# Gates of a sparse expert layer kept column by column in groups of 16 tokens: matmuls write PSUM with a step of four, and the gates meet the activations in runs of 16

## The chip, the cores and the metric

The kernel runs on one core of a Trainium2 chip. The metric is the device time of one execution in microseconds, the median of several runs. A core has TensorE (PE, with its weight loads shown apart as PEld), VectorE (DVE), ScalarE (ACT), GpSimd (POOL) and SyncE (SP), which here only issues transfers. The four compute engines share the on-chip memory SBUF; matmuls write to a second one, PSUM, whose banks hold 512 float32 per partition.

## The reference: what is computed

One encoder layer for 256 tokens of width 2048 in float32: a retention group and a recurrent group, cross attention to 256 memory tokens, then a sparse expert layer (PEER), and a final norm. Only the expert layer matters here:

```python
sub_scores = jnp.einsum('thcd,hckd->thck', q, sub_keys)     # 8 heads, 2 x 128 keys
vals, ids = lax.top_k(sub_scores, 16)
top_sc, pos = lax.top_k(cand.reshape(t, 8, 256), 16)        # cand: all sums of two of them
eid = i1 * 128 + i2                                         # 128 experts for each token
gate = jax.nn.softmax(top_sc, axis=-1)
act = jax.nn.gelu(jnp.einsum('td,tkd->tk', xb, u_tab[eid]))
out = jnp.einsum('tk,tkd->td', gate * act, v_tab[eid])
```

There are 128 x 128 = 16384 experts, each with one row of `u_tab` and one of `v_tab`. A token uses 128 of them.

## The kernel before

The kernel computes the expert layer in two ways at once. The first 96 of 128 groups of experts (`RD` = 96, regrouped by key pair) are computed densely for all 256 tokens: for each expert the activation of every token, times a gate that is zero where the token did not choose the expert. The other 32 groups are computed by gathering only the chosen rows from DRAM. The dense part is cut into 12 chunks (`NCH`) of eight groups, which makes 8 x 128 experts a chunk, experts on the partitions.

*The bank of gates.* `gbuild` makes the gates for all experts of the dense part. It takes four tokens at a time. DVE writes two comparisons with a row of numbers, `o1` (128 entries by 128 first keys, line 876) and `o2` (128 entries by 96 groups, line 879), and ACT scales `o2` by the softmax weights (line 882). For each of the four tokens PE multiplies the two (line 892): the result, 128 partitions by 96 groups, is the token's gate for every dense expert. The four results fill 384 columns of one PSUM bank, token after token, so a column's place is (token, chunk, group in chunk). A copy takes them to the SBUF tile `gs`, which collects 16 tokens in the order (chunk, token, group); ACT and DVE take turns at the copies (line 894). After 16 tokens POOL issues one DMA of `gs` to the DRAM tensor `gd` (line 898), which holds for each chunk and partition 256 tokens by 8 groups. The matmuls are plain float32, which PE runs as two passes, so 256 of them leave 512 records. The last write of `gd` is issued at 1218 us.

*Where it runs.* `gbuild` and `compact` (which picks the rows to gather) are generators. They are pumped a little after each weight step while the first chunks' U products run (`u_chunk`, PE lines 129 and 131). A scheduler orders the instructions there.

*U and V steps.* From about 1200 us a hand-written list of steps rules (`run`). A U step multiplies half a block of `u_tab` with all tokens; two give the activations of one group, which go through `foldu` (ACT line 978, DVE line 982) and gelu (ACT line 987) into the tile `act` of the chunk. A V step multiplies activations with a piece of `v_tab` (lines 924, 925, 927). All weights are split in two for accuracy: ACT rounds the raw tile to `hi` (line 1048), DVE subtracts to get `lo` (line 1054), and line 131 or 927 uses `lo`. Chunks are computed six ahead (`LEAD`): for i = 0 to 5, sixteen V steps of chunk i are followed by sixteen U steps of chunk i + 6; then come the V steps of chunks 6 to 10 alone; `v_final` does chunk 11.

*The gates' steps.* `prep_steps` puts two steps per chunk into this list, one for each half of the tokens. Each loads 128 tokens' gates of the chunk from `gd` into a raw tile, as any weight is loaded (six tiles in turn, issued by SP, eight steps ahead, line 1043), and then DVE multiplies the activations by them in place (`gate`, line 1002). For this the tile, stored (token, group), is read as (group, token). Afterwards ACT and DVE split the gated activations into two (`ah`, `al`, or `xe`; lines 1016 and 1020) for PE.

*Gathered experts.* Between the steps `chosen` is pumped with a rate of 1.17 per step: POOL gathers rows (line 1094), and DVE takes dot products with them (line 1111) or adds multiples of them to the output `hh` (line 1119). Within one engine all of this is one fixed order, so a late instruction holds up all behind it.

Of the kernel before, what the change touches and what calls it, by code (L numbers as in the profile page):

```python
# [9 lines left out]
F32 = mybir.dt.float32  # L10
# [4 lines left out]
ALU = mybir.AluOpType  # L15
AX = mybir.AxisListType

P = 128
D = 2048
KB = D // P  # L20
T = 256
# [12 lines left out]
RD = 96  # L34
RS = P - RD
NS = RS * P
NCH = RD // 8
# [34 lines left out]
def hybrid_layer_kernel(ctx: ExitStack, tc: tile.TileContext, a: dict, out: bass.AP, dbg=None):  # L72
    nc = tc.nc
    V, A, G, PE = nc.vector, nc.scalar, nc.gpsimd, nc.tensor
# [6 lines left out]
    dp = ctx.enter_context(tc.tile_pool(name="dp", bufs=1, space=bass.MemoryType.DRAM))  # L81
# [11 lines left out]
    def bigx(name):  # L93
        return b8.tile([P, KB, 2 * T], F32R, tag="X", name=name, bufs=1)

    def slot(tag, shape, name, dt=F32):
        return b8.tile(shape, dt, tag=tag, name=name, bufs=3 if tag == "ms" else 2)
# [5 lines left out]
    def sm(name):  # L103
        return ps2_.tile([P, 512], F32, tag="sm", name=name)
# [307 lines left out]
    for i in range(3):  # L412
        t = slot("qs" if i == 0 else "ms", [P, TT, 1024], "qkv"[i])
# [448 lines left out]

    ring = []
    acts = {}
    gd = dp.tile([NCH, P, T, 8], F32, name="gd")

    def gbuild():
        prev = None
        gs = None
        for n in range(T // 4 + 1):  # L870
            nxt = None
            tt, t0 = divmod(4 * n, P)
            ss = slice(t0, t0 + 4)
            if n < T // 4:
                o1 = pgt.tile([P, 4, P], F32, tag="o1", name="o1", bufs=2)
                V.tensor_tensor(o1, iota[:, None, :].to_broadcast([P, 4, P]),
                                i1T[tt][:, ss, None].to_broadcast([P, 4, P]), op=ALU.is_equal)
                o2 = pgt.tile([P, 4, P], F32, tag="o2", name="o2", bufs=2)
                V.tensor_tensor(o2[:, :, :RD], iota[:, None, :RD].to_broadcast([P, 4, RD]),
                                rT[tt][:, ss, None].to_broadcast([P, 4, RD]), op=ALU.is_equal)  # L880
                for j in range(4):
                    A.activation(o2[:, j, :RD], o2[:, j, :RD], AF.Copy, scale=gtT[tt][:, t0 + j:t0 + j + 1])
                nxt = (o1, o2)
                yield 0.9
            if prev:
                o1, o2 = prev
                m = n - 1
                if m % 4 == 0:
                    gs = slot("qs", [P, NCH, 16, 8], "gs")
                pt = sm("G")  # L890
                for j in range(4):
                    PE.matmul(pt[:, j * RD:(j + 1) * RD], o1[:, j, :], o2[:, j, :RD], start=True, stop=True)  # L892
                g0 = 4 * (m % 4)
                (V.tensor_copy if m % 2 else A.copy)(
                    gs[:, :, g0:g0 + 4, :], pt[:, :4 * RD].rearrange("p (t c x) -> p c t x", t=4, x=8))
                if m % 4 == 3:
                    tl = slice(4 * m - 12, 4 * m + 4)
                    G.dma_start(gd[:, :, tl, :].rearrange("q p t c -> p q t c"), gs)
                yield 0.4
            prev = nxt  # L900
        done.add("gbuild")
# [95 lines left out]
    def prep_steps(i):  # L997
        box = []

        def gate(g, tt):  # L1000
            av = acts[i][:, :, tt * P:(tt + 1) * P]
            V.tensor_tensor(av, g.rearrange("p (t c) -> p c t", c=8), av, op=ALU.mult)

        def rounded(k):
            if k == 0:
                if NCH - LEAD < i < NCH - 1:
                    if "x" not in spare:
                        spare["x"] = bigx("xe").rearrange("p a b -> p (a b)").rearrange(
                            "p (n c e t) -> p n c e t", n=2, c=2, e=8)
                    box.extend((spare["x"][:, i % 2, 0], spare["x"][:, i % 2, 1]))  # L1010
                else:
                    box.append(tp.tile([P, 8, T], F32R, tag="ah", name="ah"))
                    box.append(tp.tile([P, 8, T], F32R, tag="al", name="al"))
                ahs[i] = box
            s = slice(4 * k, 4 * k + 4)
            A.copy(box[0][:, s], acts[i][:, s])

        def left(k):
            s = slice(4 * k, 4 * k + 4)
            V.tensor_tensor(box[1][:, s], acts[i][:, s], box[0][:, s].bitcast(F32), op=ALU.subtract)  # L1020

        for tt in range(TT):
            post = {}
            if tt == 1:
                post = {2: [(lambda: rounded(0), None)], 4: [(lambda: rounded(1), lambda: left(0))],
                        6: [(None, lambda: left(1))]}
            yield gd[i, :, tt * P:(tt + 1) * P, :].rearrange("p t c -> p (t c)"), lambda g, tt=tt: gate(g, tt), post

    def woven(main, extra, first, apart):
        main, extra = list(main), list(extra)  # L1030
# [267 lines left out]
    pgt = pg.__enter__()  # L1298
    done.add("pb")
    wv.add(turns(gbuild(), compact()))  # L1300
    wv.rate = RB
    for i in range(LEAD):
# [12 lines left out]
    wv.rate = RC  # L1315
    wv.add(chosen(blocks_of(0, 0, BASE) + blocks_of(1, 0, BASE), True))
    steps = woven(list(u_steps(LEAD - 1))[2 * CUT:], prep_steps(0), 6, 3)
    for i in range(NCH - 1):
        if i + LEAD < NCH:
            steps += woven(v_steps(i), [], 0, 0)  # L1320
            steps += woven(u_steps(i + LEAD), prep_steps(i + 1), 3, 4)
        else:
            steps += woven(v_steps(i), prep_steps(i + 1), 2, 4)
# [98 lines left out]
```

## Time and profile before

| | |
|---|---|
| median of 3 runs | 2084.04 us (2079.66 to 2085.44) |
| profiled execution | 2085.37 us, span 2083.4 us, granted clock 0.991 |
| busy over the span | PE 97%, PEld 82%, DVE 81%, ACT 49%, POOL 18% |
| gate matmuls, line 892 | 512 passes, 67.5 us busy, 272 ns mean |
| copies out of the bank, line 894 | DVE 32 of 551 ns, ACT 32 of 475 ns |
| gate multiplies, line 1002 | 24 of 2140 ns, 51.3 us of DVE |
| issue to landing | gates out 5.3 us, gates in 8.5 us, V tiles 7.4 us (medians) |

The page gives busy times for a whole span of unlike stretches, so the views by stretch and the waits inside a stretch say more. "Idle" of an engine is put down to what released it last. The matmuls are pipelined: a row's duration is longer than the distance from one start to the next, and the distance is the pace.

### The profile page before, as it was taken

To read this page: it belongs to the slowest core of one execution; us is meant where nothing else is said; L and a number is where in the kernel's file an instruction comes from. 1 tells how busy PE (TensorE), PEld (TensorE's weight loads), DVE (VectorE), ACT (ScalarE), POOL (GpSimd) and SP (SyncE) were. 2 spreads that over 40 slices of the span, in tenths; PEclk is the share of its full clock that TensorE was granted. 3 is DMA by queue.
4 is the path that set the end of the run, shared out by engine and by line. 5 is a ranking of instruction groups with operands and counts; after the bars stand their busy time and mean duration, and the time that the engine had idled before them with its cause. 6 is when DMAs were issued, how large, how long until landed. Compare 5 with 4: busy or idle time off the path is not lost.

```text
span 2083.4 us, 28880 instructions
## 1 busy us (share of the span) xinstructions
PE 2022.8 (97%) x10416; PEld 1717.1 (82%) x10416; DVE 1694.3 (81%) x2461; ACT 1031.2 (49%) x1570; POOL 375.4 (18%) x210
## 2 busy tenths in 40 slices
PE   8999999999999999999999988999999999999998
PEld 6888878888888888888789976888888888878776
DVE  6859766644554457999988888999999999999985
ACT  6565434544544455554558853435444453534443
POOL 0200020000000000000011022333433333534531
PEclk9999999999999999999999999999999999999999
DMA  8675645566654458555576579999999999999984
GB/s 288 235 242 173 215 132 185 172 191 188 190 172 142 142 182 284 171 176 180 162 255 207 181 266 349 403 392 397 375 351 340 388 390 387 387 393 351 336 303 132
DMA packets 132933, 541.94 MB, mean 260 GB/s; under 512 B 16677, under 2 KB 19365, under 8 KB 114597
## 3 DMA queue, kind: packets, MB, share of 16 engines
q1 hardware_dynamic: 108000, 387.90, 54.9%
q0 software_dynamic: 24784, 152.16, 18.8%
q8 instruction: 81, 1.33, 0.3%
q14 instruction: 68, 0.55, 0.1%
HBM read 537.80 MB, written 18.87 MB: 267 GB/s over the span
## 4 chain that ended last, share of the span: by engine, by line
PE 80%; DVE 12%; DMA 5%; issue 2%; ACT 1%; POOL 0%; SPq 0%; ACTq 0%; DVEq 0%; POOLq 0%
PE U L129 14%; PE U L131 7%; PE wb L129 7%; PE xc L171 6%; PE xc L172 6%; PE xc L174 6%; PE acc L927 6%; PE acc L925 5%; PE acc L924 5%; PE wb L131 4%; DVE lo L120 3%; PE G L892 2%; PE V L927 2%; DMA raw<-in_V_dram 2%; PE V L924 2%
## 5 line engine op out<-in xcount | busy, mean ns | idle before, releaser
L120 DVE TENSOR_TENSOR lo<-raw,hi 128x1024 fp32r<-128x1024 f32 x384 | 470.8, 1228 | 262.7 <-PE xc L174 118.4
L119 ACT CAST hi<-raw 128x1024 fp32r<-128x1024 f32 x384 | 403.1, 1051 | 305.0 <-PE xc L172 170.4
L1048 ACT CAST hi<-raw 128x1024 fp32r<-128x1024 f32 x284 | 296.2, 1049 | 261.8 <-DMA raw<-in_V_dram 100.9
L129 PE MATMUL U<-xn,hi 128*128 128x512 f32 x1536 | 404.6, 400 | 9.6 <-ACT hi L1048 4.2
L1054 DVE TENSOR_TENSOR lo<-raw,hi 128x1024 fp32r<-128x1024 f32 x284 | 341.4, 1221 | 29.1 <-ACT hi L1048 14.2
L129 PEld LDWEIGHTS U<-xn,hi 128*128 128x128 f32 x1536 | 279.1, 191 | 61.0 <-DVE foldu L982 6.5
L131 PEld LDWEIGHTS U<-xn,lo 128*128 128x128 f32 x1536 | 211.0, 192 | 20.9 <-DVE lo L120 5.5
L131 PE MATMUL U<-xn,lo 128*128 128x256 f32 x1536 | 220.1, 285 | 3.2 <-DVE lo L120 3.2
L1094 POOL DMA_INDIRECT gat<-in_Us_dram,idx x65 | 118.9, 1829 | 232.9 <-DVE gat L1111 218.2
L925 PE MATMUL acc<-hi,al 128*128 128x512 f32 x384 | 150.7, 393 | 7.3 <-DVE al L1020 7.3
L924 PE MATMUL acc<-hi,ah 128*128 128x512 f32 x384 | 151.3, 394 | 0.0
L1111 DVE SCALAR_TENSOR_TENSOR gat<-gat,h 128x2048 f32<-128x2048 f32 x65 | 148.5, 2285 | 0.0
L129 PE MATMUL wb<-hT,hi 128*128 128x512 f32 x448 | 119.8, 400 | 0.0
L1094 POOL DMA_INDIRECT gat<-in_Vs_dram,idx x40 | 81.5, 2038 | 125.8 <-DVE hh L1119 115.9
L927 PE MATMUL acc<-lo,ah 128*128 128x512 f32 x384 | 103.5, 392 | 0.0
L1094 POOL DMA_INDIRECT h<-in_Vs_dram,idx x30 | 81.3, 2709 | 102.4 <-DVE hh L1119 94.6
L129 PE MATMUL wb<-xT,hi 128*128 128x512 f32 x368 | 93.0, 394 | 1.2 <-ACT hi L119 1.2
L1119 DVE SCALAR_TENSOR_TENSOR hh<-gat,coef,hh 128x2048 f32<-128x2048 f32 x40 | 93.9, 2347 | 0.0
L129 PEld LDWEIGHTS wb<-hT,hi 128*128 128x128 f32 x448 | 81.3, 189 | 14.0
L925 PEld LDWEIGHTS acc<-hi,al 128*128 128x128 f32 x384 | 72.8, 189 | 23.8 <-DVE al L1020 8.2
L673 POOL DMA_DIRECT2D hn<-h x2 | 1.3, 658 | 487.3 <-DVE h L671 487.3
L927 PEld LDWEIGHTS acc<-lo,ah 128*128 128x128 f32 x384 | 72.7, 189 | 15.4 <-issue 0.2
(413 smaller groups left out, 3740.9 us busy)
## 6 DMA issues: line engine op xcount, KB each, us to landing
raw<-in_U_dram SPq DMA_DIRECT2D x192, 512.0 KB, 5.3
raw<-in_V_dram SPq DMA_DIRECT2D x192, 512.0 KB, 7.4
raw<-in_w_xyg_dram SPq DMA_DIRECT2D x48, 512.0 KB, 4.3
raw<-in_w_qkv_dram SPq DMA_DIRECT2D x48, 512.0 KB, 4.3
raw<-in_w_xk_dram SPq DMA_DIRECT2D x32, 512.0 KB, 3.6
raw<-in_w_xv_dram SPq DMA_DIRECT2D x32, 512.0 KB, 4.2
raw<-in_w_out_dram SPq DMA_DIRECT2D x32, 512.0 KB, 4.0
raw<-in_w_xq_dram SPq DMA_DIRECT2D x32, 512.0 KB, 3.5
```

Of the source, the lines that this page charges most:

```text
L119: A.copy(hi, raw)
L120: V.tensor_tensor(lo, raw, hi.bitcast(F32), op=ALU.subtract)
L129: PE.matmul(pt, hi[:, ks], xt[:, kb, :], start=(kb == 0), stop=(kb == KB - 1))
L131: PE.matmul(pt[:, :T], lo[:, ks], xt[:, kb, :T], start=False, stop=False)
L171: PE.matmul(pt, xh, hi[:, w], start=(n == 0 and k == 0), stop=False)
L924: PE.matmul(pt, ah[:, c, t_], hi[:, w], start=(first and c == 0), stop=False)
L925: PE.matmul(pt, al[:, c, t_], hi[:, w], start=False, stop=False)
L927: PE.matmul(pt, ah[:, c, t_], lo[:, w], start=False, stop=(last and c == 7))
L1048: A.copy(his[t], raws[t])
L1054: V.tensor_tensor(los[t], raws[t], his[t].bitcast(F32), op=ALU.subtract)
L1094: G.indirect_dma_start(gat, None, a[tab], bass.IndirectOffsetOnAxis(ap=idx[tt][:, k:k + 1], axis=0), bounds_check=NS - 1, oob_is_err=False)
L1111: V.scalar_tensor_tensor(gat, gat, 1.0, h[0], op0=ALU.mult, op1=ALU.mult, accum_out=dots[tt, k0][:, k:k + 1])
```

## The change

Three access patterns change, and with them the layout of the bank in PSUM, SBUF and DRAM. The four products of a bank are interleaved: token j of a matmul writes columns j, j + 4, j + 8 and so on, so a column's place in PSUM is now (chunk, group, token). The copy reads the 384 columns in a row, and writes four tokens at a time into `gs`, which is now (chunk, group, token of 16). `gd` holds for each chunk and partition 16 groups of tokens, each 8 groups of experts by 16 tokens. A gate multiply therefore reads its gates in runs of 16 neighbouring tokens; activations and output keep their places.

```diff
-    gd = dp.tile([NCH, P, T, 8], F32, name="gd")
+    gd = dp.tile([NCH, P, T // 16, 8, 16], F32, name="gd")
...
-                    gs = slot("qs", [P, NCH, 16, 8], "gs")
+                    gs = slot("qs", [P, NCH, 8, 16], "gs")
                 pt = sm("G")
                 for j in range(4):
-                    PE.matmul(pt[:, j * RD:(j + 1) * RD], o1[:, j, :], o2[:, j, :RD], start=True, stop=True)
+                    PE.matmul(pt[:, :4 * RD].rearrange("p (c t) -> p c t", t=4)[:, :, j], o1[:, j, :],
+                              o2[:, j, :RD], start=True, stop=True)
                 g0 = 4 * (m % 4)
                 (V.tensor_copy if m % 2 else A.copy)(
-                    gs[:, :, g0:g0 + 4, :], pt[:, :4 * RD].rearrange("p (t c x) -> p c t x", t=4, x=8))
+                    gs[:, :, :, g0:g0 + 4], pt[:, :4 * RD].rearrange("p (c x t) -> p c x t", t=4, x=8))
                 if m % 4 == 3:
-                    tl = slice(4 * m - 12, 4 * m + 4)
-                    G.dma_start(gd[:, :, tl, :].rearrange("q p t c -> p q t c"), gs)
+                    G.dma_start(gd[:, :, m // 4].rearrange("q p c t -> p q c t"), gs)
...
         def gate(g, tt):
-            av = acts[i][:, :, tt * P:(tt + 1) * P]
-            V.tensor_tensor(av, g.rearrange("p (t c) -> p c t", c=8), av, op=ALU.mult)
+            av = acts[i][:, :, tt * P:(tt + 1) * P].rearrange("p c (b t) -> p c b t", t=16)
+            V.tensor_tensor(av, g.rearrange("p (b c t) -> p c b t", c=8, t=16), av, op=ALU.mult)
...
-            yield gd[i, :, tt * P:(tt + 1) * P, :].rearrange("p t c -> p (t c)"), lambda g, tt=tt: gate(g, tt), post
+            yield (gd[i, :, 8 * tt:8 * tt + 8].rearrange("p b c t -> p (b c t)"),
+                   lambda g, tt=tt: gate(g, tt), post)
```

The order of the instructions on each engine stays as it was. Only the form of the copies out of the bank differs, as in this piece of DVE's order while the bank is built (`gs` is the collecting tile, `G` the bank; line numbers after this place are higher by one):

```order
 L767 MAX sel<-work 128x8
 L734 TENSOR_REDUCE rt<-eq 128x32
-L894 COPY gs<-G 128x12x32
+L895 COPY gs<-G 128x96x4
 L745 TENSOR_TENSOR rr<-rt 128x128
 L768 MATCH_REPLACE work<-sel,work 128x128
```

Before, the copy writes 12 runs of 32 elements; now 96 runs of four.

## The prediction

> **What bounds the kernel now.** I read the busy shares first, then the busy time by stretch, then the chain of waits, and last the timelines of the stretches that the gates touch.
>
> ```profile
> PE 2022.8 (97%) x10416; PEld 1717.1 (82%) x10416; DVE 1694.3 (81%) x2461; ACT 1031.2 (49%) x1570; POOL 375.4 (18%) x210
> ```
>
> PE carries the whole, so a shorter instruction on DVE is worth only what PE idles for DVE. The bank of gates is built from 1030 to 1220 us, and the gates meet the activations from 1220 us on. Busy time by stretch (length; PE, PEld, DVE, ACT, POOL; granted clock, DMA share, GB/s):
>
> ```profile
> 1030.00:1220.00 190.00, 181.78 (x1217) 165.28 (x1215) 163.02 (x340) 137.01 (x367) 23.67 (x22) 0.99 0.63 199
> ...
> 1268.00:1660.00 392.00, 392.00 (x1959) 333.30 (x1958) 377.18 (x398) 173.56 (x220) 134.48 (x72) 1.00 0.97 373
> 1660.00:1795.00 135.00, 134.57 (x706) 114.43 (x705) 131.87 (x128) 61.18 (x84) 45.63 (x24) 1.00 0.98 388
> 1795.00:2000.00 205.00, 198.87 (x859) 159.60 (x858) 203.23 (x176) 85.44 (x87) 105.25 (x38) 1.00 0.96 360
> ```
>
> From 1268 to 1660 us PE never rests. From 1795 to 2000 us DVE is busy for 203 of 205 us, and PE has gaps. Their size is read from PE's pace. In the chain of waits the blocks of U steps begin with these rows (start, length):
>
> ```profile
> 1306.16 1.81 PE U L129 x8
> ...
> 1394.37 1.81 PE U L129 x8
> ...
> 1659.43 1.81 PE U L129 x8
> ...
> 1748.83 1.81 PE U L129 x8
> ```
>
> An undisturbed round of 16 V and 16 U steps takes 1394.37 - 1306.16 = 88.21 us. The round from 1659 takes 89.40, so 1.2 us are lost. The timeline of PE gives the rest:
>
> ```profile
> 1794.29 0.40 PE L924 MATMUL acc<-hi,ah 128*128 128x512 f32 x1
> ...
> 1796.12 1.07 PE L927 MATMUL acc<-lo,ah 128*128 128x512 f32 x4
> ...
> 1798.84 1.07 PE L927 MATMUL acc<-lo,ah 128*128 128x512 f32 x4
> ...
> 1847.63 1.21 PE L927 MATMUL acc<-lo,xe 128*128 128x512 f32 x4 [1.04 <-DVE lo L1054]
> ...
> 2022.71 0.47 PE L924 MATMUL acc<-hi,ah 128*128 128x512 f32 x1
> ```
>
> A V step takes 1798.84 - 1796.12 = 2.72 us. The U block from 1748.83 ends at 1794.29, after 45.5 us, where 88.21 - 16 x 2.72 = 44.7 would do: 0.8 lost. Then come five chunks of V alone, 80 steps or 217.6 us, which take 2022.71 - 1794.29 = 228.4: 10.8 lost. After 1659 us PE thus loses 12.8 us. What it waits for, from 1800 to 2010 us (total, times, longest):
>
> ```profile
> ACT hi L1048 <- DMA raw<-in_V_dram: 77.7, 42, 6.3
> ...
> PE acc L927 <- DVE lo L1054: 3.4, 6, 1.0
> ...
> PE V L927 <- DVE lo L1054: 2.7, 5, 0.9
> ```
>
> PE waits for the low halves that DVE makes and for nothing else; ACT waits for loads, but has time to spare. DVE's timeline shows what stood ahead of the half that was late at 1847.63, a gate multiply (line 1002):
>
> ```profile
> 1844.25 2.19 DVE L1002 TENSOR_TENSOR act<-raw,act 128x1024 f32<-128x1024 f32 x1
> 1846.36 1.22 DVE L1054 TENSOR_TENSOR lo<-raw,hi 128x1024 fp32r<-128x1024 f32 x1
> ```
>
> **The change, part by part.** No instruction is added, removed or moved on any queue; access patterns differ, so each term is a count times a change of duration.
>
> *The gate multiplies.* From the groups of instructions, 1220 to 2010 us (count, busy us, mean ns):
>
> ```profile
> L1054 DVE TENSOR_TENSOR lo<-raw,hi 128x1024 fp32r<-128x1024 f32 x277 | 333.0, 1221 | 26.8 <-ACT hi L1048 14.2 <-issue 9.1 <-PE acc L927 3.4
> ...
> L1002 DVE TENSOR_TENSOR act<-raw,act 128x1024 f32<-128x1024 f32 x24 | 51.3, 2140 | 0.9 <-DMA raw<-gd 0.9
> ```
>
> Both read two tensors of 1024 elements. The gate's first operand steps by eight elements (32 bytes), and that costs it 919 ns. Afterwards that operand comes in runs of 16. The same view for 1030 to 1222 us has an instruction that reads such runs (line 733), and rows for the terms below:
>
> ```profile
> L129 PE MATMUL U<-xn,hi 128*128 128x512 f32 x345 | 99.4, 411 | 5.0 <-DVE foldu L982 4.0 <-ACT hi L119 1.0
> ...
> L131 PE MATMUL U<-xn,lo 128*128 128x256 f32 x344 | 52.0, 289 | 1.2 <-DVE lo L120 1.2
> ...
> L876 DVE TENSOR_TENSOR o<-iota,trio 128x512 f32<-128x512 f32 x62 | 42.3, 683 | 0.0
> ...
> L894 DVE COPY gs<-G 128x384 f32<-128x384 f32 x32 | 17.6, 551 | 2.9 <-PE G L892 2.9
> ...
> L894 ACT COPY gs<-G 128x384 f32<-128x384 f32 x32 | 15.2, 475 | 10.9 <-PE G L892 10.8
> ...
> L733 DVE TENSOR_TENSOR eq<-eq,rt 128x512 f32<-128x512 f32 x4 | 2.7, 679 | 0.0
> ```
>
> Line 733 takes 679 ns for 512 elements, no more than line 876 (683). Bounds for the new gate: 1221 ns and the old 2140; I take 1221, since a row has the very run length. That saves 0.92 us a gate, 22 us of DVE over 24. Where the gates stand:
>
> ```profile
> 1268.00:1660.00 392.00, 17.18 (x8) 1.00 0.97 373
> 1660.00:1795.00 135.00, 8.63 (x4) 1.00 0.98 388
> 1795.00:2000.00 205.00, 21.44 (x10) 1.00 0.96 360
> ```
>
> The eight before 1660 save 7.4 us of DVE under a PE that is full: nothing. The four up to 1795 free 3.7 us where PE loses 1.2 + 0.8 = 2.0; I take 1.6. The ten of the V-only part free 9.2 us where PE loses 10.8. DVE's 203.2 us there become 194.0; the same 205 us hold 205/228.4 of the 80 steps, 71.8, which PE does in 195.3: the two are then level. Stalls from other bursts stay, so I take 8.0 back, bounds 4 and 9.2. What is late next is PE itself. The loads come earlier with the rows they replace, and must keep up: 360 GB/s over 205 us is 73.8 MB, and in 197 us that is 375 GB/s, under the 388 that the stretch before it moved with PE at 134.6 of 135 us.
>
> The two first gates lie at the start of the stage, where loads are late. There SP's queue, DVE and PE show:
>
> ```profile
> 1234.39 3.36 SPq L1043 DMA_DIRECT2D raw<-in_V_dram  x2
> ```
> ```profile
> 1235.38 2.01 DVE L1002 TENSOR_TENSOR act<-raw,act 128x1024 f32<-128x1024 f32 x1 [0.69 <-DMA raw<-gd]
> ```
> ```profile
> 1265.60 0.80 PE L925 MATMUL acc<-hi,al 128*128 128x512 f32 x1 [4.76 <-DVE al L1020]
> ```
>
> The second V load leaves SP at 1237.75, just after the second gate has freed its buffer at 1237.39; hd's two loads queue behind it. A gate 0.9 us shorter lets these go up to 0.9 us sooner. Bounds 0 and 0.9; I take 0.5.
>
> *The bank written in steps of four.* No matmul of this kernel writes its bank with a step, so the price is bounded from neighbours. The gate matmuls, 256 in two passes each, beside one of 256 columns (min/median/max ns), and 16 passes in the chain:
>
> ```profile
> L892 PE MATMUL G<-o,o x512: 243/275/421, 1034.5 to 1214.8; 128*128 128x96 f32 x171
> ```
> ```profile
> L583 PE MATMUL xs<-kv,qx x64: 377/379/381, 610.4 to 703.7; 128*128 128x256 f32 x64
> ```
> ```profile
> 1124.93 1.76 PE G L892 x16
> ```
>
> A column of these costs (379 - 243)/160 = 0.85 ns, so 96 columns stream for 82 ns, but a pass takes 1.76/16 = 110 ns: 28 ns are slack. Lower bound: nothing. Upper bound: each lone column costs twice, as a lone element did in the old gate; the stream becomes 164 ns, each pass 54 ns longer, 512 x 54 = 27.6 us on a PE that is busy for 181.8 of 190 us there. I take nothing: line 129 against 131 shows (411 - 289)/256 = 0.48 ns a column, so banks already take columns almost twice as fast as these matmuls bring them, and half that pace would still serve 0.85 ns.
>
> [...]
>
> *The copies out of the bank* (line 894). The source becomes contiguous; the destination falls into runs of four. Bounds: 0, and twice the pace per element as in the old gate, 384 x 0.9 = 0.35 us each, 11 us on DVE and about as much on ACT. Against PE's 181.8 us DVE has 163 and ACT 137 in these 190, so even 11 is covered; if the cover went, it would cost those 11. I take 0.
>
> *DMA.* Both transfers of the bank keep their runs, 512 bytes into DRAM and 4 KB out: 0.
>
> Sum: 8.0 + 1.6 + 0.5 = 10.1 us less. The profiled execution took 2085.4 us (span 2083.4), 1.3 above the median of the three runs, 2084.0. So 2075.3 for it, and **2074** as a median.
>
> **The rivals.** *Stepped bank writes slow the matmuls* (slower). It decides once a pass outgrows its 110 ns; PE in the bank stretch has no gaps to take it up. [...] Against it: the 28 ns of slack and the low column rate. At 27.6 us, 2084.0 + 27.6 - 10.1 = 2101; with half the price 2088. *Another wait takes the place of DVE in the V-only part*: loads, already waited for by ACT for 77.7 us, become late for DVE too, or stalls come from bursts that are not gates. For it: DMA share 0.96 to 0.98; against it: 388 GB/s held PE full just before. With 3 to 5 us recovered, 2079 to 2081. *The gate is not faster*, because 64 bursts of 16 cost as much as steps did: 2084; line 733 speaks against it.
>
> **How the numbers follow.** Forecast 0.56, with its own range 2070 to 2079 (recovery 5 to 14, the latter if all 12.8 us and the start come back); the matmul rival 0.23, the other wait 0.16, no faster gate 0.05. A measurement of this kernel tells 0.3%, 6.3 us, from no change: below 2077.8 is faster, above 2090.3 slower. Of the forecast nearly all lies below, 0.52; the rest of it and the two small cases make 0.25; slower 0.23, nearly all of the matmul rival. The range must reach into that rival to leave out less than 2 in 10: 2070 to 2101.
>
> **What would show it.** Line 1002 at about 1220 ns (wrong: near 2140). A chain of 16 gate passes still at 1.76 us, and the bank stretch no longer than before (wrong: 2.6 us, and U's first chunk later by over 20). Line 894 within 0.1 us of 551 and 475. The five V-only chunks in about 220 us, with PE's waits for line 1054 mostly gone, and DVE idle. The forecast is wrong if the gate rows shrink while the V-only part keeps its 228 us, or if the bank stretch grows.

## The result, and the profile after

The changed kernel takes 2074.16 us (median; 2070.80 to 2077.89), the kernel before, measured beside it, 2086.41 us (2079.66 to 2090.82). The ratio is 0.9945, with a 95% interval of 0.9928 to 0.9961: 11.5 us faster (8.1 to 15.0), beyond the 0.3% that the prediction took as the least that can be told. The profiled execution took 2072.02 us, with a span of 2070.2 us and a granted clock of 0.991, as before.

First the operations that the change touches. The views of two tiles, the activations and the bank of gates, give count, min/median/max ns, first and last start:

```profile
L1002 DVE TENSOR_TENSOR act<-raw,act x24: 1218/1224/1231, 1223.7 to 1975.8; 128x1024 f32<-128x1024 f32 x24
```
```profile
L892 PE MATMUL G<-o,o x512: 243/275/350, 1034.0 to 1214.8; 128*128 128x96 f32 x171
L895 ACT COPY gs<-G x32: 453/479/485, 1035.0 to 1212.6; 128x384 f32<-128x384 f32 x32
L895 DVE COPY gs<-G x32: 542/551/559, 1039.1 to 1216.5; 128x384 f32<-128x384 f32 x32
```

A gate multiply fell from 2143 to 1224 ns (medians of this view in both kernels). The gate matmuls, which now write with a step of four, keep their 243 and 275 ns; the copies, which now write runs of four, take 551 ns on DVE and 479 on ACT, where the same view of before has 550 and 480. The pace counts for PE, not the duration of a row, so the chain of waits is read at the same place:

```profile
1124.94 1.76 PE G L892 x16
```

Sixteen passes still take 1.76 us. The first load of the list of steps leaves SP at 1214.30 us, at 1214.29 before: the bank stretch has the same length.

Then the rounds. In the chain of waits the blocks of U steps now begin here:

```profile
1299.81 1.81 PE U L129 x8
1388.02 1.81 PE U L129 x8
...
1652.66 1.81 PE U L129 x8
1740.87 1.81 PE U L129 x8
```

All five distances are 88.21 or 88.22 us, the round from 1652 us too, which took 89.40 before: 441.06 us together against 442.67. And the first block begins 6.35 us earlier.

The timeline of PE shows the part with V alone, with one of its stalls:

```profile
1785.38 0.40 PE L924 MATMUL acc<-hi,ah 128*128 128x512 f32 x1
...
1818.76 1.20 PE L927 MATMUL acc<-lo,ah 128*128 128x512 f32 x4 [1.24 <-DVE lo L1055]
...
2009.55 0.47 PE L924 MATMUL acc<-hi,ah 128*128 128x512 f32 x1
```

It takes 2009.55 - 1785.38 = 224.2 us, 228.4 before. The last U block takes 1785.38 - 1740.87 = 44.5 where it took 45.5. The waits from 1800 to 2010 us (total, times, longest) and the busy times by stretch say what is left there:

```profile
ACT hi L1049 <- DMA raw<-in_V_dram: 78.0, 40, 5.3
...
DVE lo L1055 <- ACT hi L1049: 4.4, 4, 2.2
...
PE acc L927 <- DVE lo L1055: 2.7, 5, 1.2
...
PE V L927 <- DVE lo L1055: 0.3, 1, 0.3
```
```profile
1260.00:1652.00 392.00, 391.79 (x1964) 333.36 (x1963) 373.79 (x397) 175.04 (x221) 125.38 (x73) 1.00 0.98 380
1652.00:1783.00 131.00, 131.00 (x693) 112.99 (x693) 127.29 (x129) 60.76 (x81) 38.67 (x24) 1.00 0.99 392
1783.00:1990.00 207.00, 203.89 (x890) 165.08 (x890) 200.00 (x181) 87.37 (x90) 84.81 (x40) 1.00 0.95 366
```

PE's waits for the low halves are halved, 3.0 us for 6.1, but they are not gone. DVE, busy for 203 of 205 us before, is still busy for 200 of 207; PE's 203.9 of 207 are now level with it. ACT waits for loads as before. The stall at 1818.76 has no gate directly ahead of it: on DVE's timeline the late halves stand behind a multiply-add of the gathered experts (line 1120), and between 1797 and 1807 us DVE had waited 3.8 us for ACT's `hi`:

```profile
1815.22 2.35 DVE L1120 SCALAR_TENSOR_TENSOR hh<-h,coef,hh 128x2048 f32<-128x2048 f32 x1
1817.49 2.35 DVE L1055 TENSOR_TENSOR lo<-raw,hi 128x1024 fp32r<-128x1024 f32 x2
```

Where the time went, stage by stage, in the profiled executions of both (each number is a distance between two rows of the timelines or of the chain of waits; for the second pair both kernels were profiled again):

| stage (us) | before | after | before again | after again |
|---|---|---|---|---|
| up to SP's first load of the list of steps | 1214.3 | 1214.3 | 1219.1 | 1214.9 |
| from there to the first U block of the chain | 91.9 | 85.5 | 90.4 | 85.6 |
| five rounds of V and U | 442.7 | 441.1 | 442.7 | 441.6 |
| last U block | 45.5 | 44.5 | 45.5 | 44.5 |
| V alone | 228.4 | 224.2 | 228.5 | 223.7 |
| rest | 60.7 | 60.7 | 60.7 | 60.6 |
| span | 2083.4 | 2070.2 | 2086.9 | 2070.9 |

The three stages after the first U block give 6.8 us in the first pair and 6.9 in the second. Another 6.4 and 4.9 (from the unrounded rows) lie in the start, where the prediction had put 0.5 (the 4.2 us ahead of it in the second pair are not there in the first). This is what the experiments had to settle.

### The profile page after: what moved, and what is told of

It reads as the page before. It is cut to its first block, busy times and chain, and to the rows that moved or that the text cites. A ratio compares the mean times of both kernels' runs of the same rounds, so it can differ in the third digit from the quotient of the medians.

```text
span 2070.2 us, 28880 instructions
## 1 busy us (share of the span) xinstructions
PE 2019.8 (98%) x10416; PEld 1718.8 (83%) x10416; DVE 1674.2 (81%) x2461; ACT 1032.3 (50%) x1570; POOL 334.8 (16%) x210
## 4 chain that ended last, share of the span: by engine, by line
PE 80%; DVE 13%; DMA 4%; issue 2%; ACT 1%; POOL 0%; ACTq 0%; SPq 0%; DVEq 0%; POOLq 0%
PE U L129 14%; PE wb L129 7%; PE U L131 7%; PE xc L171 6%; PE xc L172 6%; PE xc L174 6%; PE acc L927 6%; PE acc L925 6%; PE acc L924 6%; PE wb L131 4%; DVE lo L120 4%; PE G L892 2%; PE V L927 2%; PE V L924 2%; PE V L925 2%
## 5 line engine op out<-in xcount | busy, mean ns | idle before, releaser
L1055 DVE TENSOR_TENSOR lo<-raw,hi 128x1024 fp32r<-128x1024 f32 x284 | 342.7, 1222 | 31.8 <-issue 13.4
L1095 POOL DMA_INDIRECT gat<-in_Us_dram,idx x65 | 107.6, 1655 | 243.4 <-DVE gat L1112 229.1
L1095 POOL DMA_INDIRECT gat<-in_Vs_dram,idx x40 | 75.8, 1894 | 132.3 <-DVE hh L1120 118.9
L924 PEld LDWEIGHTS acc<-hi,ah 128*128 128x128 f32 x384 | 72.1, 188 | 15.4 <-issue 0.5
L882 ACT ACTIVATE o<-o,trio 128x96 f32<-128x96 f32 x256 | 74.0, 365 | 17.8 <-DVE o L879 17.4
```

Of the source, the lines that this page charges most:

```text
L924: PE.matmul(pt, ah[:, c, t_], hi[:, w], start=(first and c == 0), stop=False)
L1055: V.tensor_tensor(los[t], raws[t], his[t].bitcast(F32), op=ALU.subtract)
L1095: G.indirect_dma_start(gat, None, a[tab], bass.IndirectOffsetOnAxis(ap=idx[tt][:, k:k + 1], axis=0), bounds_check=NS - 1, oob_is_err=False)
```

## The experiments

Theory A: every gate saves 0.92 us, and the two at the start hold up loads that all else follows, so that their 1.8 us turn into about 6. Theory B: the gain comes from the gates in the part with V alone and in the mixed rounds just ahead of it; what the start shows is not the gates' doing. Rival C: the stepped writes or the copies cost something that another gain hides.

The first four kernels keep the new bank and give only some gates their runs of 16. The gates with the old step pair a token's activations with other gates of the same tile, so their output is not the layer's; the amount of work and of bytes is the same. The edit, with the condition that each kernel has:

```diff
-            V.tensor_tensor(av, g.rearrange("p (b c t) -> p c b t", c=8, t=16), av, op=ALU.mult)
+            if CONDITION:
+                V.tensor_tensor(av, g.rearrange("p (b c t) -> p c b t", c=8, t=16), av, op=ALU.mult)
+            else:
+                av = acts[i][:, :, tt * P:(tt + 1) * P]
+                V.tensor_tensor(av, g.rearrange("p (t c) -> p c t", c=8), av, op=ALU.mult)
```

### The bank alone, without a faster gate (condition: False)

> The new bank, copies and transfers, but all 24 gate multiplies read their gates with the old step of eight elements, so they pair gates with other tokens; the work is otherwise that of the changed kernel. Theory A (each gate saving counts where PE waits for DVE, at the start of the V and U stage too): line 1002 rows near 2140 ns and the time of the kernel before, ratio 1.000 within 0.002, since stepped writes and short runs cost nothing. Theory B (the early lead of 6.35 us at the first round is chance in when loads land): the same, 1.000. Rival C (stepped bank writes cost PE something that the faster gates hide): slower than before, 2090 us or more, ratio over 1.003.

Measured: 2084.55 us beside 2084.41, ratio 1.0002 (0.9985 to 1.0020). The views of the tiles of this kernel:

```profile
L1006 DVE TENSOR_TENSOR act<-raw,act x24: 1993/2138/2187, 1225.8 to 1984.5; 128x1024 f32<-128x1024 f32 x24
```
```profile
L892 PE MATMUL G<-o,o x512: 243/275/422, 1033.5 to 1217.0; 128*128 128x96 f32 x171
L895 ACT COPY gs<-G x32: 453/479/487, 1035.3 to 1214.8; 128x384 f32<-128x384 f32 x32
L895 DVE COPY gs<-G x32: 537/551/559, 1040.2 to 1218.7; 128x384 f32<-128x384 f32 x32
```

With all gates slow again the new bank costs nothing that can be measured, and nothing was hidden: rival C falls. The interval allows a cost of at most 0.2%, 4 us, where the rival of the prediction had 27.6.

But its start is short too. Here are the waits of PE for `al` in the timelines, first this kernel's, then the changed one's; both answer to the 4.76 us that the prediction showed of before at 1265.60 us:

```profile
1264.40 0.50 PE L925 MATMUL acc<-hi,al 128*128 128x512 f32 x1 [0.21 <-DVE al L1024]
```
```profile
1261.62 0.50 PE L925 MATMUL acc<-hi,al 128*128 128x512 f32 x1 [0.21 <-DVE al L1020]
```

The wait is gone with slow gates as with fast ones. So in the profiled execution this kernel's first U block comes 86.1 us after its first load, and its span is 2079.8 us, although its median is that of before.

What is late there is a load. DVE makes `al` in its fixed order, and in the kernel before a low half ahead of it waits 4.41 us for ACT's `hi`; ACT in turn waits for a tile of `v_tab`. ACT's timelines, first of before, then of this kernel:

```profile
1258.38 1.05 ACT L1048 CAST hi<-raw 128x1024 fp32r<-128x1024 f32 x1 [7.35 <-DMA raw<-in_V_dram]
```
```profile
1256.81 1.04 ACT L1053 CAST hi<-raw 128x1024 fp32r<-128x1024 f32 x1 [2.44 <-DMA raw<-in_V_dram]
```

The kernel before reaches its first V step 37.8 us after the first load, sooner than the changed kernel with 39.6; but from there to the first U block it takes 54.0 us, and the changed kernel 45.9. The waits for `al` make up most of these 8.1 us; and behind the long one PE's granted clock is 0.50 from 1265.5 to 1270 us, where the changed kernel has 1.00.

### Only the first chunk's two gates (condition: i == 0)

> As the changed kernel, but only the two gates of chunk 0 read in runs of 16; the other 22 read with the old step (and so pair gates with other tokens). Theory A: these two, in the stretch where loads are late, give the 6 us by which the first U block of the long rounds came earlier: ratio about 0.997, first such block near 1300 us. Theory B: at most 1 us, ratio 0.9995 to 1.000, and where that block starts varies from execution to execution by some us with no tie to the gates.

Measured: 2082.59 us beside 2084.41, ratio 0.9992 (0.9978 to 1.0006): 1.7 us less, between 4.6 less and 1.2 more. Theory A's 6 us are outside.

### All but the first chunk's gates (condition: i > 0)

> As the changed kernel, but the two gates of chunk 0 read with the old step (and pair gates with other tokens); 22 read in runs of 16. Theory A: 6 us less gain than the changed kernel, ratio about 0.997. Theory B: the whole gain but for at most 1 us, ratio about 0.995.

Measured: 2074.55 us beside 2084.41, ratio 0.9947 (0.9927 to 0.9966). Without the first two gates the whole gain is there. Theory A falls from this side too.

### Only the last ten gates, those of the part with V alone (condition: i >= 7)

> As the changed kernel, but only the ten gates of the last five chunks, which stand among V steps alone, read in runs of 16; the others read with the old step (and pair gates with other tokens). Theory A: 4 to 5 us, as the two profiles differ in that part (228.4 against 224.2 us), ratio about 0.998. Theory B: most of the gain, 8 us as predicted, ratio about 0.996, since those gates stand where DVE is full.

Measured: 2075.76 us beside 2084.41, ratio 0.9959 (0.9941 to 0.9977): 8.5 us less (4.8 to 12.3), most of the gain. Its timeline of PE has the two ends of the part with V alone at 1789.68 and 2012.54, which makes 222.9 us, 5.6 less than before. The chain of waits begins its last blocks of U steps here:

```profile
1654.78 1.81 PE U L129 x8
...
1744.21 1.81 PE U L129 x8
```

With slow gates ahead the round from 1655 us again takes 89.43 us, and not 88.21: the 1.2 us there are the work of that round's own gates, as the prediction had it.

### Gates shrunk to 128 of 1024 elements

Each gate multiplies only the first 16 of its 128 tokens, 128 of 1024 elements as the rows below show. The other activations go on without gates, so that work is left out.

```diff
-            V.tensor_tensor(av, g.rearrange("p (b c t) -> p c b t", c=8, t=16), av, op=ALU.mult)
+            g4 = g.rearrange("p (b c t) -> p c b t", c=8, t=16)
+            V.tensor_tensor(av[:, :, 0], g4[:, :, 0], av[:, :, 0], op=ALU.mult)
```

> As the changed kernel, but each gate multiply treats only one of 16 tokens' groups, so nearly all activations stay without a gate; DVE is freed of another 24 x 1.0 us. Theory B (DVE bounds the part of V steps alone until it meets PE's 217.6 us): that part falls from some 223.5 to 218 to 220 us, and the whole by 4 us against the changed kernel, ratio to the kernel before 0.992 to 0.993. Rival (loads or the other bursts of DVE hold that part): no further gain, 0.9945 as the changed kernel.

Measured: 2071.68 us beside 2084.66, ratio 0.9946 (0.9925 to 0.9968). The tile of the activations and the ends of the part with V alone on PE's timeline:

```profile
L1003 DVE TENSOR_TENSOR act<-raw,act x24: 280/284/292, 1224.1 to 1970.8; 128x128 f32<-128x128 f32 x24
```
```profile
1786.24 0.40 PE L924 MATMUL acc<-hi,ah 128*128 128x512 f32 x1
...
2006.72 0.47 PE L924 MATMUL acc<-hi,ah 128*128 128x512 f32 x1
```

Ten gates that are again 0.94 us shorter shorten the part to 220.5 us, 3.7 less than after the change, and leave 2.9 of loss over the 217.6 us that 80 steps need. So after the change 3.7 of the 6.6 us still lost there go with the gates, and 2.9 don't. (The three other profiles with these ten gates fast take 222.8 to 223.7 us; against them it is 2.3 to 3.2.) The first 0.92 us a gate brought 4.2, the next 0.94 us 3.7. The rounds take 441.07 us, as after the change. The whole time can't be told from that of the changed kernel, so the stage speaks against the rival, and the time can't decide.

### What a gate costs by the length of its runs, and stepped writes where PE has no slack

In one kernel the chunks take six forms of reading the gates in turn: runs of 16, 8, 4 and 2 tokens, lone elements 32 bytes apart, and all in a row (the last five pair gates with other tokens). And the score matmuls of the cross attention, two results of 256 columns to a bank, write it with a step of two, so that their readers read with a step:

```diff
-                PE.matmul(pt[:, tt * T:(tt + 1) * T], qx[kb // 8][:, kb % 8, tt * P:(tt + 1) * P],
+                PE.matmul(pt.rearrange("p (t s) -> p s t", s=TT)[:, tt], qx[kb // 8][:, kb % 8, tt * P:(tt + 1) * P],
...
+            elif i % 6 == 3:
+                av = acts[i][:, :, tt * P:(tt + 1) * P].rearrange("p c (b t) -> p c b t", t=2)
+                V.tensor_tensor(av, g.rearrange("p (b c t) -> p c b t", c=8, t=2), av, op=ALU.mult)
```

> A look at the disputed costs by themselves, on the changed kernel. The gate multiplies of chunks 0 to 11 read their gates in runs of 16, 8, 4, 2, 1 (the old step of eight) and, last, as one contiguous row, in turn (all but the first form pair gates with other tokens); and the score matmuls of the cross attention (line 583 before, plain float32, 256 columns) write their bank with a step of two. Theory (a lone element costs a second slot, a pair or more does not): runs of 16, 8 and 4 at 1.22 us, runs of 2 between 1.2 and 1.7, single elements 2.14, contiguous 1.22; the stepped score matmuls as before, 379 ns a pass, since plain float32 brings a column only every 0.85 ns. [...]

Measured in one execution, of 2074.71 us, by the tile of the activations (in this order: runs of 16, 8, 4, 2, lone elements, all in a row), by the tile of the scores, and in the chain of waits:

```profile
L1003 DVE TENSOR_TENSOR act<-raw,act x4: 1219/1221/1226, 1222.5 to 1753.9; 128x1024 f32<-128x1024 f32 x4
L1006 DVE TENSOR_TENSOR act<-raw,act x4: 1212/1218/1219, 1301.3 to 1796.4; 128x1024 f32<-128x1024 f32 x4
L1009 DVE TENSOR_TENSOR act<-raw,act x4: 1216/1218/1220, 1389.5 to 1844.3; 128x1024 f32<-128x1024 f32 x4
L1012 DVE TENSOR_TENSOR act<-raw,act x4: 1209/1215/1222, 1479.3 to 1888.3; 128x1024 f32<-128x1024 f32 x4
L1015 DVE TENSOR_TENSOR act<-raw,act x4: 2139/2144/2147, 1566.0 to 1934.5; 128x1024 f32<-128x1024 f32 x4
L1018 DVE TENSOR_TENSOR act<-raw,act x4: 1218/1218/1222, 1656.9 to 1978.5; 128x1024 f32<-128x1024 f32 x4
```
```profile
L583 PE MATMUL xs<-kv,qx x64: 377/379/381, 608.7 to 702.0; 128*128 128x256 f32 x64
...
L590 ACT ACTIVATE xp<-xs,xm,rsc x8: 553/560/567, 614.8 to 704.2; 128x256 f32<-128x256 f32 x8
...
L586 DVE TENSOR_REDUCE xm<-xs x4: 691/691/692, 612.4 to 702.4; 128x2 f32<-128x512 f32 x4
```
```profile
608.86 3.46 PE xs L583 x16
```

There are two prices and nothing between them in the forms tried: runs of 16, 8, 4 and 2 take 1215 to 1221 ns, a row without gaps 1218, and only lone elements take 2144, 0.92 us more than runs of 16. Why a pair is enough, these rows don't show.

The score matmuls keep the 379 ns that the prediction showed for columns written in a row. Sixteen take 3.46 us, 216 ns each, which is what 256 columns of 0.85 ns stream for (218) and twice the 110 ns of a gate pass: here no slack hides a slower write. Written in a row they take 3.46 us as well, in the kernel before. So these plain float32 matmuls show no slowing from a stepped write, neither with a step of two (3.46 us for 16) nor with one of four (1.76 us for 16 gate passes). For the faster columns of line 131 a stepped write wasn't tried, and it stays open.

### A faster pump

If DVE has time to spare, more of the gathered experts could be done early. The rate of `chosen`, 1.17 per step, is raised in the changed kernel, all else as it is:

```diff
-RA, RB, RC = 1.1, 2.35, 1.17
+RA, RB, RC = 1.1, 2.35, 1.21
```

> The changed kernel with the gathered experts pumped a little faster, 1.21 instead of 1.17 per step, so that some four of their tasks move from the V steps alone into the mixed rounds, where DVE now idles for 18 of 392 us. If DVE still bounds the V part: 4 x 2.3 = 9 us less DVE there, 3 us faster than the changed kernel, ratio about 0.993. If loads bound the mixed rounds (DMA share 0.98): nothing, 0.9945, or slower.

> The same with 1.25: seven tasks move, 16 us of DVE, about what the mixed rounds have to spare. If DVE bounds the V part alone: the part at PE's pace, 5 us faster than the changed kernel, ratio about 0.992; if the mixed rounds become DVE's or the loads': PE loses there what it wins later, 0.994 to 0.997.

Measured: with 1.21 a ratio of 0.9994 (0.9981 to 1.0007) to the kernel before, with 1.25 one of 1.0013 (1.0000 to 1.0026). Both lose the whole gain. PE's timeline of the kernel with 1.21, and a stretch of the windows of the one with 1.25, show where:

```profile
1264.74 0.80 PE L925 MATMUL acc<-hi,al 128*128 128x512 f32 x1 [4.77 <-DVE al L1020]
```
```profile
1661.00:1753.00 92.00, 88.87 (x449) 75.18 (x448) 88.09 (x91) 39.81 (x51) 28.79 (x18) 1.00 1.00 397
```

The wait of the start is back at 1.21, 4.77 us, although the gates are fast; at 1.25 it is 4.14. So it goes neither with the gates nor with the bank alone. It goes with the late load: ACT's longest wait for a tile of `v_tab` between 1240 and 1264 us is 7.35 and 6.67 us in the two profiles of before, 6.63 and 6.17 at these two rates, and at most 2.71 in the ten other profiles. What makes that load late, the gathers that now start earlier or something else, is not shown. At 1.25 the round from 1661 us takes 92.2 us and not 88.2; PE is busy for 88.9 of 92 us, with a DMA share of 1.00 at 397 GB/s. With V alone the two take 227.7 and 225.5 us, more than the 224.2 of the changed kernel.

### A slower pump, and both kernels again

The rate 1.14 in the same place, and beside it the changed kernel and the kernel before unaltered:

> The changed kernel with the gathered experts pumped at 1.14 instead of 1.17 per step. Pumping faster lost 10 to 13 us, at the start, in the mixed rounds and among V steps alone. If that came from loads that compete with the gathers: slower pumping relieves all three, 2 to 5 us faster than the changed kernel, ratio 0.992 to 0.9935. If DVE bounds the V part, it gets three tasks or 7 us more to do there: 2 to 5 us slower, 0.996 to 0.997. If it came from the order in which tasks and other DVE work fall: anything between.

> The changed kernel itself once more, beside the next one on one chip, with a second profile. Theory B (the V steps alone give 4 to 8 us, the mixed rounds 2.6, the start up to 1.7): ratio 0.9945 within 0.0015; the last U block's end to the last chunk 222 to 225 us, the five distances between U blocks 441.1 us, and the first U block anywhere from 1298 to 1304 us.

> The kernel before, for a second profile. Both theories: the part of V steps alone 228 us, the five distances between U blocks 442.7 us; theory B: the first U block between 1298 and 1306 us, without a tie to the gates.

Measured: the changed kernel 2073.63 us beside 2087.41, ratio 0.9936 (0.9920 to 0.9952), so the result holds; with 1.14 a ratio of 0.9953 (0.9937 to 0.9970), no better. Its part with V alone takes 220.5 us, but the timeline of PE behind it has

```profile
2010.62 2.08 PE L927 MATMUL acc<-lo,ah 128*128 128x512 f32 x4 [6.46 <-DVE lo L120]
```

What the slower pump saves in one part it loses as one wait in the next. The kernel before again took 2089.31 us in its one execution, with a start of 90.4 us and the wait for `al` at 4.06: the two profiles of before agree on it. No other rate of the pump beats the changed kernel.

### The bank alone, again

All profiles with the new bank and a rate of 1.17 had a short start, both profiles of before a long one, yet the bank alone had gained no time. So it was run a second time, to see whether its start is long in another execution.

> The kernel of the first experiment once more (new bank and copies, all gates with the old step), for a second profile of its start. From SP's first load of the list of steps to the first U block of the mixed rounds the kernel before took 91.9 and 90.4 us in two profiles, the kernels with the new bank 85.2 to 88.2 in eight, whatever their first gates did. If the new bank itself brings that: 85 to 88 us again, and a ratio to the kernel before of 0.998 or less. If it is chance of the execution: anywhere from 85 to 92 us, and a ratio of 1.000.

Measured: 2087.06 us beside 2085.04, ratio 1.0007 (0.9990 to 1.0025): no gain, as in the first run. And its start is short again: 86.4 us from the first load to the first U block. But the lead is lost later, in a place where none of the edits is. POOL's timelines of the same kernel's first execution and of this one, at the same gather:

```profile
1989.16 1.73 POOL L1179 DMA_INDIRECT gat<-hn,spti  x1 [1.71 <-DVE hh L1124]
...
1992.56 4.00 POOL L1179 DMA_INDIRECT gat<-in_Us_dram,spi  x1 [1.67 <-DVE hh L1124]
```
```profile
1989.01 13.07 POOL L1179 DMA_INDIRECT gat<-hn,spti  x1 [1.71 <-DVE hh L1124]
2002.38 3.09 POOL L1179 DMA_INDIRECT gat<-in_Us_dram,spi  x1 [0.30 <-issue]
```

Behind the 13.07 us the next gather begins at 2002.38 and not at 1992.56, 9.8 us later. DVE waits 5.83 us for its rows, and PE, on its own timeline, waits for a low half that is queued behind DVE's dot product:

```profile
2017.35 1.68 PE L927 MATMUL acc<-lo,xe 128*128 128x512 f32 x4 [4.68 <-DVE lo L1059]
```

The part with V alone takes 235.9 us in this execution, 7.5 more than in the first of the same kernel. The kernel with only the first two gates fast had the same: a gather of 13.07 us, a wait of 5.17 on PE, and 236.0 us. In the other profiles with a rate of 1.17 that gather takes 1.73 or 1.74 us.

What follows, and what doesn't: the short start shows in all profiles with the new bank at 1.17, whatever the gates' speed, and brings the bank alone no time. A long gather in part of its executions could take it back, 7.5 us for about 5; that would fit both profiles of the bank alone, but the timed executions show no stages, so it is argued and not shown. At 1.17 the long gather was seen in two of the five profiles whose last ten gates are all slow, and in none of the five where those are fast or shrunk; if fast gates avoid it, that would be part of the change's gain, but these are too few to tell. Nor need the long start be in every execution of the kernel before. Its two profiles take 869.1 and 867.8 us from SP's first load to the end, and in none of the fourteen profiles does that load leave before 1212.4 us. An execution like either would have a span of 2080.2 us or more, but 23 of the 79 executions of the kernel before that were timed beside the experiments have a shorter one, down to 2075.5 us. Why the start differs from before is open as well: the new bank moves no instruction and no byte, and at 1.21 the long start came back with that same bank.

## Why the prediction was right

The forecast was 2074 us, faster; measured were 2074.16 and, again, 2073.63. Its mechanism stands: a shorter gate, with the time of the bank unchanged, worth what PE waits for DVE late in the expert layer. The times say whose gain it is: the bank alone gives nothing, the last ten gates 8.5 us, all but the first two 11.0, all of them 11.5. That the sum came out so near is partly luck, since two of its terms were off in opposite directions by the profiles.

- *A gate falls to 1221 ns.* Right: 1224. To read line 733's runs of 16 against line 876 was enough, and the runs could have been eight times shorter (1215 ns in runs of two).
- *The stepped writes cost nothing.* Right, against the rival with 0.23: passes at 1.76 us for 16, ratio 1.0002 with the bank alone. The rival's 27.6 us took over for PE's columns the price of a lone element in the old gate; no run shows that price on PE. Of the two reasons, the 28 ns of slack that the prediction estimated in a pass weren't needed, at least for a step of two: the score matmuls, at 216 ns each for columns that stream for 218, have none and kept 379 ns. The other reason was worked out wrongly: half the pace of line 131's columns is 0.96 ns a column, which would not serve one every 0.85 ns. At 0.96 the score matmuls would have taken 246 ns each, and they took 216; so a stepped write is faster than that. Whether a faster stream of columns would pay for the step, no run shows.
- *The copies and the transfers cost nothing.* Right: 551 and 479 ns, and a bank stretch that ends at the same time.
- *The eight gates before 1660 us give nothing.* As far as the two profiles go, right but for 0.4 us: the first four rounds take 352.85 us after and 353.27 before.
- *The four up to 1795 us give 1.6 of the 2.0 lost.* Slightly low: the round from 1652 us gained 1.2 and the last U block 0.95, together 2.1; with the 0.4 above, 2.6. The kernel with only the last ten gates lost the 1.2 again.
- *The ten with V alone give 8.0 of 10.8.* By the profiles this is the term that was mis-sized: 4.2 and 4.9 us in the two pairs, 5.6 with those ten alone, in the lower part of its bounds of 4 to 9.2. The step that failed is "stalls from other bursts stay, so I take 8.0 back": it left 2.8 us of loss, and 6.6 were found. It was worked out that PE and DVE would then be level, and they are, 203.9 and 200.0 of 207 us; but that did not end PE's waits, and DVE is not idle, as the signs had it. The gates, at little over half their price, still are part of the bursts: the shrunk gates took another 2.3 to 3.7 us out, and 2.9 stay without them. The times of the last ten alone, 8.5 us less, are wide enough (4.8 to 12.3) to hold both numbers.
- *The two gates at the start give 0.5.* For the gates that fits: 1.7 us (-1.2 to 4.6) with them alone, and the whole gain without them. So do the profiles with the new bank at 1.17: their start takes 85.2 to 86.3 us where the first two gates are fast or shrunk (five), and 86.1 to 88.2 where they are slow (four), about 1 us apart in the mean. But against the two profiles of before 6.4 and 4.9 us show in that stretch, which the prediction's "bounds 0 and 0.9" exclude. It had looked at one chain, from the second gate over its buffer to the loads, and not asked whether the wait of 4.76 us for `al` would be there in other executions or with slow gates under a new bank. Behind that wait is a late load of `v_tab`; why it is late stays open.
- *The rival of another wait taking DVE's place* held in part. DVE now waits for ACT's `hi`, and so for loads, 4.4 us between 1800 and 2010 us, in the row shown above, where the same view of before has

```profile
DVE lo L1054 <- ACT hi L1048: 0.6, 1, 0.6
```

  What was not recovered is 2.4 to 3.8 of the 8.0 us; how much of it is this wait and how much the gates' own bursts was not separated. It took a part of the term, not the forecast.

The three stages that the gates reach add up to 6.8 and 6.9 us. By the times the change gives 11.5 (8.1 to 15.0) and 13.4 (10.0 to 16.7). The differences, 4.7 and 6.5 us, are of the size of the start's, which the bank alone couldn't turn into time. So the gain is the gates' by the times, but where these 4.7 and 6.5 us arise stays open. Whether the changed kernel keeps the start's lead because it is free of the long gather can't be told from two of its profiles.

## What to carry to other kernels

Price a strided operand by the length of its runs, from rows of the same kernel: for these gates on DVE in float32 two neighbours were enough (1215 ns, and 1218 for a row without gaps), and only lone elements, 32 bytes apart, cost 1.76 times as much (2144). When a stretch has one engine full and another nearly so, don't book the whole of the bound engine's relief (here, by the profiles, 4.2 to 5.6 of the 8.0 us came back), and find the rest by shrinking the same instruction further. And when a stage differs between two profiles by more than the edit can explain, run a kernel that has the edit's bystanders alone before the difference is booked as its gain.

## What the runs showed of the hardware that was not expected

DVE has two prices for a gate and no slope between them in the forms tried: 1215 to 1221 ns for runs of 2, 4, 8, 16 and a whole row, 2144 ns for lone elements 32 bytes apart. The plain float32 matmuls wrote PSUM with a step of two at the same 379 ns for 256 columns, and with a step of four at the same 110 ns a pass; the readers of a bank with a step of two, a reduce on DVE (691 ns) and an exponential on ACT (560 ns), cost what they cost on whole rows (692 and 561 before). An indirect gather on POOL that takes 1.73 us in the other profiles at the same rate took 13.07 us in two profiled executions, to the hundredth the same in both, and then cost PE about 5 us; what sets it off is not known.
